# Block sums of the normalised x1 made before its transposition, all FFN-in tiles as seven block products

## The chip, the cores and the metric

The program runs on one core of one Trainium2 chip. The metric is the device time of one execution in microseconds. Engines: PE (TensorE), DVE (VectorE), ACT (ScalarE), POOL (GpSimd), SP (SyncE, which issues the DMAs here).

## What is computed

One encoder layer with 1024 tokens, model width 1024 and hidden width 2816, all fp32. The part of the reference that the change touches begins where the mixers (`mix`: four matrix-memory heads and eight window-attention heads) are done:

```python
x = _layer_norm(ALPHA * x + mix, ln1_g, ln1_b)          # x1
gate_ff, up_ff = jnp.split(x @ w_ffn_in, 2, axis=-1)
ffn = (jax.nn.silu(gate_ff) * up_ff) @ w_ffn_out
ple = jax.nn.sigmoid(x @ w_ple_gate) * (p_i @ w_ple_proj)
return _layer_norm(ALPHA * x + ffn + ple, ln2_g, ln2_b)
```

with `mix = concat(heads) @ w_out`, ALPHA = 2^(1/4) and `_layer_norm(x, g, b) = (x - mean) / sqrt(var + 1e-5) * g + b` over the 1024 columns.

## The kernel before, in words

Every matrix product is exact to fp32 by pieces: an operand is split into a high part (cast by ACT to fp32r, `..h` or `..hi`) and a low part (the remainder, subtracted by DVE or POOL, `..l` or `..lo`), and `mm3` (L110) issues three PE products, high x high, high x low and low x high. All products of this part have 512 columns. `split` makes the parts of one tile (L89); `load_w` loads a weight and splits it.

Stages, in order of time: projections and the two kinds of heads; the output projection (`out_proj`, PSUM banks named `yo`), which adds to eight token tiles y of 128x1024; the first norm; the FFN's inward products; the gate with its embedding product; the FFN's outward products; the second norm.

The output projection runs in two halves: the attention half under the last heads, the other at their end, 12 PE products for each token tile and half of the columns. After the second half of a tile, `ln1_norm` (L711) takes its statistics, ACT normalises, DVE multiplies by g1, POOL adds b1 (L722), and y goes to DRAM as `yd`, from where it is read again at the gate. `ln1_tr` (L726) transposes the tile on PE, 128x128 pieces into a bank `x1t`, eight for a token tile, and splits four columns' blocks into `x1h` and `x1l` (L741, L742).

The inward products have 22 tiles of 128 hidden columns (gate and up). The first two (NPL = 2) are plain: `ffn_plain` (L812), 16 products x 3 for each half of the tokens, 96 a tile, PSUM banks `fi`. The other twenty use a 2 x 2 block scheme (rows: halves of the tokens; inner: halves of x1's columns) with seven block products, 84 PE products a tile (`ffn_wino`, L881). Its operands are the blocks b11, b21, b22 of x1 itself, four block sums t1 to t4 that are made once, and sums of weight blocks that are made for each tile (`wino_w`, pieces a1 to a4). The sums t1 to t4 come from `diff` (L830): three DVE or POOL instructions of 128x1024 on the high and low parts already made, a cast and a remainder, beside the plain tiles' products. The results go to hidden blocks `ya` to `yd`, summed and written to DRAM for the outward stage; `weight_sums` (L791) does the like for the outward weights.

The gate is a seven-product scheme too, in the order 1, 2, 7, 6, 5, 3, 4 (MORDER). Its weight pieces `g<m><q>` come from raw tiles `wpg` by `piece` (L975), in products 3, 5, 6 and 7 after a sum of two raw tiles (`block_sum`, L970: q = 0 on DVE, q = 1 on POOL). `embed` (L1016) multiplies the embedding pieces `pu` (`p0`, `p1`) and `wu` (`wpp0`, `wpp1`) into one of three PSUM banks `plp` and has DVE multiply and add to the y read again.

Within an engine instructions run in program order; a scheduler sets that order when the program is built, by dependences and its own estimate of the time, so that the code's order is only a start. SBUF tiles come from tagged pools (X: 16 of 4 KB a partition; Y: 8; F4: 16; `raw`: 2; `whi`, `wlo`: 4), and a tile waits for the last reader of the slot that it takes.

## Time and profile before

| | |
|---|---|
| median of 3 runs | 1291.14 us (1290.29 to 1291.2) |
| the profiled execution | 1289.46 us, span in the trace 1287.7 us |
| PE busy | 1232.6 us (96%), 5985 products |
| DVE, ACT, POOL busy | 853.8, 510.6, 404.9 us |
| mean granted clock | 0.982 of full speed |

The span is the time from the first to the last record of the trace; the profiled execution is a little longer than it. A row of a timeline has the start, the duration, the engine and line, the operation, and in brackets how long the engine was idle before it and what ended that. A product of 512 columns is listed with 0.39 us, but products overlap: the distance of two starts is what each takes of PE's time.

### The profile page before, as it was taken

What the parts mean: (1) busy time and instruction counts of PE and PEld (TensorE: products, weight loads), DVE (VectorE), ACT (ScalarE), POOL (GpSimd) and SP (SyncE); (2) the same over time, 40 slices, a digit from 0 to 9 for tenths busy, and PEclk for the clock granted to TensorE, in tenths of its full rate; (3) what the DMA queues carried; (4) which work ended last, traced back from release to release, by engine and by line L of the source; (5) the groups of instructions that cost most, each with busy time, mean ns of one, the idle gap of its engine ahead of it and who ended that gap; (6) DMA issues with size and microseconds to landing.
All of it is one profiled execution on the core that took longest, in us unless ns stands there. A gap on an engine that the chain in (4) does not pass through costs nothing.

```text
span 1287.7 us, 16350 instructions
## 1 busy us (share of the span) xinstructions
PE 1232.6 (96%) x5985; PEld 1015.9 (79%) x5985; DVE 853.8 (66%) x1512; ACT 510.6 (40%) x906; POOL 404.9 (31%) x292
## 2 busy tenths in 40 slices
...
GB/s 240 115 36 66 46 54 50 151 34 87 90 177 221 49 102 111 34 106 130 173 203 188 167 130 212 172 188 166 161 136 199 165 179 229 180 191 197 151 1 131
DMA packets 67744, 174.39 MB, mean 135 GB/s; under 512 B 6288, under 2 KB 11088, under 8 KB 67664
## 3 DMA queue, kind: packets, MB, share of 16 engines
...
## 4 chain that ended last, share of the span: by engine, by line
PE 76%; DVE 12%; DMA 4%; POOL 3%; issue 2%; ACT 2%; SPq 1%; POOLq 0%; ACTq 0%; DVEq 0%
PE ma L113 5%; PE ma L111 5%; PE ma L112 5%; PE mc L111 3%; PE mc L112 3%; PE mc L113 3%; PE op L491 2%; PE oa L113 2%; PE oa L111 2%; PE oa L112 2%; PE ob L113 2%; PE ob L112 2%; PE ob L111 2%; PE pj_qk L111 2%; PE pj_qk L112 2%
## 5 line engine op out<-in xcount | busy, mean ns | idle before, releaser
L926 DVE TENSOR_TENSOR us<-us,ma 128x512 f32<-128x512 f32 x20 | 13.7, 686 | 103.3 <-PE ma L113 92.6
L1142 POOL TENSOR_TENSOR rs<-rs,mhalf 128x1 f32<-128x1 f32 x8 | 9.4, 1184 | 224.8 <-DVE rs L1141 224.6
L466 POOL TENSOR_SCALAR e<-e,st 128x384 f32<-128x384 f32 (+1 forms) x64 | 36.1, 577 | 119.2 <-DVE st L464 96.0
L865 POOL TENSOR_TENSOR s<-ru,rg 128x512 f32<-128x512 f32 x19 | 26.2, 1377 | 147.5 <-DMA ru<-in_wffi_dram 136.9
L462 ACT ACTIVATE e<-e,st 128x384 f32<-128x384 f32 (+1 forms) x64 | 37.2, 582 | 39.6 <-DVE st L458 39.5
L111 PE MATMUL yo<-hi_wo,mh 128*128 128x512 f32 x128 | 50.7, 396 | 1.9 <-DVE y L662 1.0
L111 PE MATMUL pj_qk<-xh,hi_qk 128*128 128x512 f32 x128 | 50.9, 398 | 0.0
L112 PE MATMUL pj_qk<-xl,hi_qk 128*128 128x512 f32 x128 | 50.9, 398 | 0.0
L113 PE MATMUL pj_qk<-xh,lo_qk 128*128 128x512 f32 x128 | 50.6, 395 | 0.0
L112 PE MATMUL yo<-lo_wo,mh 128*128 128x512 f32 x128 | 50.4, 395 | 0.0
L113 PE MATMUL yo<-hi_wo,ml 128*128 128x512 f32 x128 | 50.0, 395 | 0.0
L456 DVE CUSTOM_DVE_ANT_0 e<-sp,bias 128x384 f32<-128x384 f32 (+1 forms) x64 | 32.2, 521 | 24.5 <-PE sp L455 23.3
L870 POOL TENSOR_TENSOR s<-rg,s 128x512 f32<-128x512 f32 x20 | 28.6, 1432 | 60.8 <-DVE a4l L96 60.8
L874 POOL TENSOR_TENSOR s<-ru 128x512 f32<-128x512 f32 x20 | 32.7, 1633 | 45.4 <-DVE a2l L96 45.4
L283 DVE SCALAR_TENSOR_TENSOR qk<-pre,colt,qk 128x1024 f32<-128x1024 f32 x32 | 45.9, 1435 | 0.4
L90 ACT CAST a2h<-s 128x512 fp32r<-128x512 f32 x40 | 22.9, 618 | 46.9 <-PE mc L112 46.9
L90 ACT CAST a4h<-s 128x512 fp32r<-128x512 f32 x20 | 12.4, 621 | 69.6 <-PE ma L112 40.5
L111 PE MATMUL mc<-t1h,a3h 128*128 128x512 f32 x80 | 32.3, 403 | 4.3 <-ACT a3h L90 4.3
L491 PE MATMUL op<-eT,av 128*64 128x128 f32 x352 | 34.4, 285 | 0.0
L586 POOL TENSOR_TENSOR mw<-mw,maskb 128x512 f32<-128x512 f32 x16 | 24.1, 1504 | 32.7 <-DMA mw<-mwd 32.7
L113 PE MATMUL mc<-t1h,a3l 128*128 128x512 f32 x80 | 32.2, 403 | 1.6 <-DVE a3l L96 1.6
L113 PE MATMUL ma<-t2h,a2l 128*128 128x512 f32 x80 | 31.4, 392 | 0.8 <-DVE a2l L96 0.8
...
## 6 DMA issues: line engine op xcount, KB each, us to landing
...
```

The source lines that it names most:

```text
L90: act.copy(dst_hi, src)
L111: pe.matmul(o, ah, bh, start=start, stop=False, skip_group_check=goes_on)
L112: pe.matmul(o, ah, bl, start=False, stop=False, skip_group_check=goes_on)
L113: last["mm"] = pe.matmul(o, al, bh, start=False, stop=stop, skip_group_check=goes_on)
L283: dve.scalar_tensor_tensor(y, pre[:, w:w + S], colt[:, ct, w:w + 1], y, ALU.mult, ALU.add)
L456: dve.tensor_tensor_reduce(e[:, i, :L], sp[:, :L], biasd[j][:, i, off:off + L], 1.0, -BIG, ALU.add, ALU.max, accum_out=st[:, i:i + 1])
L462: act.activation(e[:, i, :L], e[:, i, :L], AF.Exp, bias=st[:, i:i + 1], accum_out=st[:, 2 + i:3 + i])
L466: pool.tensor_scalar(e[:, i, :L], e[:, i, :L], st[:, 6 + i:7 + i], 0.0, ALU.mult, ALU.add)
L491: pe.matmul(op[i * 64:i * 64 + 64, (n % 4) * P:(n % 4 + 1) * P], av[:, k0 + kb, i * 64:i * 64 + 64], eT[:, i, kb * P:(kb + 1) * P], start= ...
L865: (dve if i == NPL else pool).tensor_tensor(s3, ru[:, lo, :], rg[:, lo, :], ALU.subtract)
L870: pool.tensor_tensor(s4, rg[:, up, :], s2, ALU.subtract)
L874: pool.tensor_tensor(s1, ru[:, lo, :], ru[:, up, :], ALU.add)
```

## The change

In the change, all 22 inward tiles are done by seven block products, the first two as well, and the plain tiles' code goes. The tiles are normalised in the order 0, 1, 4, 5, 2, 3, 6, 7. POOL no longer adds b1 to y. The bias is a column constant when x1 is transposed: `bcol` (b1 as 128 x 8, columns on partitions) is added to b11, b21, b22 and t2 in the split (ACT with a bias, DVE with an instruction that adds and subtracts), and a difference of two of its halves to t3. t1 and t4 need none, since it cancels there. The block sums are made on y itself, in place, with y1 of token tile t and y2 of tile t + 4 (`t_sums`): for tiles 0 and 1 by POOL, for tiles 2 and 3 two of four by DVE. They wait for the write of y to `yd` and for the transposes of the blocks that the same y still has to give. The sums are then transposed (`tr_block`) like the blocks. The bias is put back onto the y read again: ALPHA x b1, 16 additions of POOL in the gate's stage.

The weights of tiles 0 and 1 load during the norm. Products 1 and 2 of tile 0 are issued ahead of the late sums. Raw tiles of the outward weights move from X to F4, behind a copy that holds each back (`weight_load`). In the gate, the raw tiles of products 1 and 2 load and the pieces of product 1 are made within the last inward tile; `wpp0` and `p0` go to Y slots, `p1` and `wpp1` to X.

```diff
-NPL = 2
+TORD = (4, 5, 0, 1, 6, 7, 2, 3)
+LORD = (0, 1, 4, 5, 2, 3, 6, 7)
...
-    section("F", {"xt": 2, "fo": 3})
+    section("F", {"w": 5})
...
+    bcol = const.tile([P, 8], F32, name="bcol")
+    nc.sync.dma_start(bcol, ln1b.rearrange("o (k p) -> p (o k)", p=P))
+    bdif = const.tile([P, 4], F32, name="bdif")
+    dve.tensor_tensor(bdif, bcol[:, 0:4], bcol[:, 4:8], ALU.subtract)
...
-            pool.tensor_tensor(ys, ys, b1a[:, nh * 512:nh * 512 + 512], ALU.add)
         nc.sync.dma_start(yd[t], y)
...
+    def tr_block(ts, k0, blk, tt, bias=None, late=False):
+        s = slice(tt * P, (tt + 2) * P)
+        for q in range(2):
+            tb = pjb("x1s") if late else bank("x1t", "w")
+            for j in range(2):
+                for i, t in enumerate(ts):
+                    c = k0 + (2 * q + j) * P
+                    pe.transpose(tb[:, (2 * j + i) * P:(2 * j + i + 1) * P], ya[t][:, c:c + P], ident)
+            h, l = blk[q]
+            if bias is None:
+                tv = tb.rearrange("p (a b) -> p a b", b=2 * P)
+                act.copy(h[:, :, s], tv)
+                dve.tensor_tensor(l[:, :, s], tv, h[:, :, s].bitcast(F32), ALU.subtract)
+                continue
+            for j in range(2):
+                tv, bc = tb[:, j * 256:j * 256 + 256], bias[:, 2 * q + j:2 * q + j + 1]
+                act.activation(h[:, j, s], tv, AF.Identity, bias=bc)
+                dve.scalar_tensor_tensor(l[:, j, s], tv, bc, h[:, j, s].bitcast(F32), ALU.add, ALU.subtract)
...
+    def t_sums(tt, late=False):
...
+        for t in (tt, tt + 1):
+            y1, y2 = ya[t], ya[t + 4]
+            eng = dve if late else pool
+            eng.tensor_tensor(y2[:, lohi[1]], y2[:, lohi[0]], y2[:, lohi[1]], ALU.subtract)
+            eng.tensor_tensor(y2[:, lohi[0]], y2[:, lohi[0]], y1[:, lohi[0]], ALU.subtract)
+            pool.tensor_tensor(y1[:, lohi[0]], y1[:, lohi[0]], y2[:, lohi[1]], ALU.subtract)
+            pool.tensor_tensor(y1[:, lohi[1]], y1[:, lohi[1]], y1[:, lohi[0]], ALU.subtract)
+        tr_block((tt + 4, tt + 5), 0, bx["t1"], tt, None, late)
+        tr_block((tt + 4, tt + 5), 512, bx["t3"], tt, bdif, late)
+
+    def t_sums_late():
+        bx["t2"], bx["t4"] = new_block((X, X), "t2"), new_block((F4, X), "t4")
+        for tt in (0, 2):
+            tr_block((tt, tt + 1), 0, bx["t2"], tt, b_hi, True)
+        for tt in (0, 2):
+            tr_block((tt, tt + 1), 512, bx["t4"], tt, None, True)
...
+    for n, t in enumerate(LORD):
+        for nh in range(2):
+            list(out_proj(t, nh, (0, 1), u, False))
         ln1_norm(t)
...
+        if n in (2, 4, 6):
+            ln1_tr(LORD[n - 2])
+        if n == 3:
+            ws = [wino_w1(0, raw8), wino_w1(1, raw8f)]
+        if n == 5:
+            t_sums(0)
+    ln1_tr(6)
...
+    def weight_load(r, after):
+        if r < NPR:
+            wsr[r] = F4([P, 2, 512], F32, f"sa{r}"), F4([P, 2, 512], F32, f"sb{r}")
+            for nh in range(2):
+                dve.tensor_copy(wsr[r][nh][:, 0, 0:1], after[:, 0:1])
+                nc.sync.dma_start(wsr[r][nh], wffo[r, nh])
...
-    def ffn_plain(i, w, hf):
...
-    def diff(new, plus, minus, name, engs, stage):
...
+    bs = {1: bx["b11"], 2: bx["b21"], 3: bx["b22"], 5: bx["t1"], 7: bx["t3"]}
+    w2 = {0: wino_w2(0, *ws[0])}
+    early = [wino_a(0, ws[0][2])]
+    t_sums(2, True)
+    early.append(wino_a(1, ws[1][2]))
...
+        if i == FT - 1:
+            load_gate(0, 0, F4)
+            load_gate(0, 1, lambda shape, dt, name: staging(shape, name))
+            m1g.append(piece(wpair, rawg[0, 0][0], 2, "g10", dve))
+        wino_b(i, w, *early[i])
+        if i == FT - 1:
+            m1g.append(piece(wpair, rawg[0, 0][1], 2, "g11", dve))
...
+        if m == 2:
+            load_gate(1, 1, F4)
+            wu[0] = load_h(ypair, wpp[0], "wpp0", dve)
+            pu[0] = load_h(ypair, pT[0], "p0", dve)
+            reload(range(4), Y)
...
-        if m == 2:
-            wu[0] = load_h(fpair, wpp[0], "wpp0", dve)
-            pu[0] = load_h(fpair, pT[0], "p0", dve)
         if m == 7:
             gs["v"] = temps(F4, "pv")
-            pu[1] = load_h(fpair, pT[1], "p1", pool)
...
+            for tt in range(4):
+                add_bias(0, 0, tt)
```

`wino_a` issues products 1 and 2 of a tile, `wino_b` the other five; for tile 0 it holds, between products 5 and 6, `t_sums_late`.

What the scheduler makes of it is seen at three places. On PE, at the end of the projection (`yo`), before: the last token tile is transposed, and the plain products of the first token half follow at once.

```order
L111 MATMUL yo<-hi_wo_4322,mh_4082 128x512
L112 MATMUL yo<-lo_wo_4323,mh_4082 128x512
L113 MATMUL yo<-hi_wo_4322,ml_4083 128x512
L737 MATMUL x1t<-ident,y_4060 128x128 x8
L111 MATMUL fi<-x1h_4478,hi_fi_4834 128x512
L111 MATMUL fi<-x1h_4478,hi_fi_4841 128x512
L112 MATMUL fi<-x1l_4479,hi_fi_4834 128x512
L113 MATMUL fi<-x1h_4478,lo_fi_4835 128x512
```

After: the last product's place is taken by transposes of several tiles (y_4108 is the last but one to be normalised), and the first block products, `mb` and `ma`, read b21 and b11, with the low parts from DVE.

```order
L112 MATMUL mb<-b21h_4458,a1h_4544 128x512
L739 MATMUL x1t<-ident,y_4144 128x128
L739 MATMUL x1t<-ident,y_4160 128x128
L739 MATMUL x1t<-ident,y_4144 128x128
L739 MATMUL x1t<-ident,y_4160 128x128
L113 MATMUL mb<-b21l_4459,a1h_4544 128x512
L114 MATMUL mb<-b21h_4458,a1l_4545 128x512
L739 MATMUL x1t<-ident,y_4108 128x128
L112 MATMUL mb<-b21h_4458,a1h_4544 128x512
L739 MATMUL x1t<-ident,y_4108 128x128
L112 MATMUL ma<-b11h_4454,a1h_4544 128x512
```

The first consumers behind the projection were products of one token half with plain weights, and are now those of two blocks that hold the tiles 2 and 3.

On DVE, at the same place, before: the last normalised tiles' multiplications (L721) and splits (L742).

```order
L717 SCALAR_TENSOR_TENSOR rs_4744<-mv_4743,rs_4744 128x1
L721 TENSOR_TENSOR y_4144<-y_4144,g1a 128x512 x2
L742 TENSOR_TENSOR x1l_4703<-x1t,x1h_4702 128x2x128
L742 TENSOR_TENSOR x1l_4705<-x1t,x1h_4704 128x2x128
L742 TENSOR_TENSOR x1l_4707<-x1t,x1h_4706 128x2x128
L717 SCALAR_TENSOR_TENSOR rs_4790<-mv_4789,rs_4790 128x1
L742 TENSOR_TENSOR x1l_4709<-x1t,x1h_4708 128x2x128
L721 TENSOR_TENSOR y_4160<-y_4160,g1a 128x512 x2
L742 TENSOR_TENSOR x1l_4703<-x1t,x1h_4702 128x2x128
```

After: the low parts of b11, b21 and t3 (L749), with weight pieces (L97) and the multiplications (L725) of the tile y_4108 between them.

```order
L725 TENSOR_TENSOR y_4108<-y_4108,g1a 128x512 x2
L97 TENSOR_TENSOR a2l_4867<-s_4872,a2h_4866 128x512
L749 SCALAR_TENSOR_TENSOR b11l_4455<-x1t,bcol,b11h_4454 128x256
L718 BN_AGGR mv_4819<-st_4802 128x2
L749 SCALAR_TENSOR_TENSOR b21l_4459<-x1t,bcol,b21h_4458 128x256
L749 SCALAR_TENSOR_TENSOR t3l_4667<-x1t,bdif,t3h_4666 128x256
L749 SCALAR_TENSOR_TENSOR t3l_4669<-x1t,bdif,t3h_4668 128x256
L749 SCALAR_TENSOR_TENSOR b11l_4457<-x1t,bcol,b11h_4456 128x256
L719 TENSOR_SCALAR rs_4820<-mv_4819 128x1
L749 SCALAR_TENSOR_TENSOR b21l_4459<-x1t,bcol,b21h_4458 128x256
L749 SCALAR_TENSOR_TENSOR b21l_4461<-x1t,bcol,b21h_4460 128x256
```

Weight pieces, gain multiplications and low parts of the sums now stand in one queue ahead of the last parts of b21.

On DVE in the gate, before: three sums of raw gate tiles (L973) and a piece of product 6 stand ahead of the low parts of `p0`.

```order
L978 TENSOR_TENSOR g70lo<-wpg_8012,g70hi 128x1024
L973 TENSOR_TENSOR wpg_8012<-wpg_8012,wpg_8016 128x1024
L973 TENSOR_TENSOR wpg_8004<-wpg_8004,wpg_8012 128x1024
L973 TENSOR_TENSOR wpg_8008<-wpg_8008,wpg_8012 128x1024
L978 TENSOR_TENSOR g60lo<-wpg_8012,g60hi 128x1024
L96 TENSOR_TENSOR p0lo<-r_p_8158,p0hi 128x512
L96 TENSOR_TENSOR p0lo<-r_p_8162,p0hi 128x512
L926 TENSOR_TENSOR e_8166<-pc_8080,pg_8094 128x512
```

After: the low parts of `p0` stand ahead of the three sums (L983), and the first multiplication by `plp` (L1071) behind them.

```order
L988 TENSOR_TENSOR g70lo<-wpg_8087,g70hi 128x1024
L97 TENSOR_TENSOR p0lo<-r_p_8165,p0hi 128x512
L97 TENSOR_TENSOR p0lo<-r_p_8169,p0hi 128x512
L965 TENSOR_TENSOR e_8241<-pc_8143,pg_8189 128x512
L983 TENSOR_TENSOR wpg_8087<-wpg_8087,wpg_8149 128x1024
L983 TENSOR_TENSOR wpg_7993<-wpg_7993,wpg_8087 128x1024
L983 TENSOR_TENSOR wpg_7997<-wpg_7997,wpg_8087 128x1024
L965 TENSOR_TENSOR e_8253<-pc_8143,pg_8190 128x512
L988 TENSOR_TENSOR g60lo<-wpg_8087,g60hi 128x1024
L1071 TENSOR_TENSOR e_8241<-e_8241,plp 128x512
```

The sums and `g60lo` keep their order among themselves; the embedding pieces and one addition have moved ahead of them.

## Rows read from the trace of the kernel before

**Rows 1.** PE's timeline, first norm to first seven-product tiles: start us, us, engine line operation
```profile
454.83 0.50 PE L111 MATMUL yo<-hi_wo,mh 128*128 128x512 f32 x1 [0.26 <-DVE y L662]
...
465.89 0.39 PE L113 MATMUL yo<-hi_wo,ml 128*128 128x512 f32 x1
...
477.00 0.39 PE L111 MATMUL yo<-hi_wo,mh 128*128 128x512 f32 x1
...
494.74 1.03 PE L737 MATMUL x1t<-ident,y 128*128 128x128 f32 x8
495.53 0.48 PE L112 MATMUL yo<-lo_wo,mh 128*128 128x512 f32 x1
...
579.01 0.63 PE L111 MATMUL mc<-t1h,a3h 128*128 128x512 f32 x1
...
582.42 0.63 PE L113 MATMUL mc<-t1h,a3l 128*128 128x512 f32 x1
...
600.40 0.39 PE L111 MATMUL mc<-t1h,a3h 128*128 128x512 f32 x1
```

**Rows 2.** Windows: stretch, its us, busy (x instructions) of PE PEld DVE ACT POOL, clock, DMA
```profile
570.00:600.00 30.00, 23.38 (x88) 17.94 (x87) 27.09 (x25) 10.66 (x17) 17.31 (x8) 0.83 0.42 151
600.00:970.00 370.00, 370.00 (x1634) 306.55 (x1633) 223.70 (x286) 127.92 (x207) 109.38 (x74) 1.00 0.49 172
```

**Rows 3.** Waits of PE over the whole run: total us, times, longest us
```profile
PE plp L113 <- DVE p0lo L96: 4.5, 1, 4.5
...
PE mc L111 <- ACT a3h L90: 4.3, 1, 4.3
...
PE x1t L737 <- DVE x1l L742: 3.0, 2, 1.5
PE pg L111 <- ACT g21hi L977: 2.8, 1, 2.8
```

**Rows 4.** PE's timeline in the gate
```profile
970.09 0.39 PE L113 MATMUL pg<-g20hi,x1l 128*128 128x512 f32 x1
...
992.90 0.64 PE L113 MATMUL plp<-wpp0hi,p0lo 128*128 128x512 f32 x1 [4.55 <-DVE p0lo L96]
...
997.35 0.39 PE L111 MATMUL pg<-g70hi,t3h 128*128 128x512 f32 x1
```

**Rows 5.** Groups of POOL, 456 to 600 us: count, busy us, mean ns
```profile
L722 POOL TENSOR_TENSOR y<-y,b1a 128x512 f32<-128x512 f32 x16 | 22.4, 1414 | 10.5 <-DVE y L721 10.5
```

**Rows 6.** Groups of DVE, 456 to 600 us
```profile
L721 DVE TENSOR_TENSOR y<-y,g1a 128x512 f32<-128x512 f32 x16 | 13.8, 883 | 1.4 <-ACT y L720 1.4
L742 DVE TENSOR_TENSOR x1l<-x1t,x1h 128x256 fp32r<-128x256 f32 x32 | 12.7, 412 | 4.5 <-ACT x1h L741 4.3
...
L662 DVE TENSOR_TENSOR y<-y,yo 128x512 f32<-128x512 f32 x15 | 10.2, 683 | 5.2 <-PE yo L113 5.1
L838 DVE TENSOR_TENSOR t1s<-t1s,x1l 128x1024 f32<-128x1024 f32 x2 | 6.7, 3412 | 0.0
...
L96 DVE TENSOR_TENSOR a1l<-rg,a1h 128x1024 fp32r<-128x1024 f32 x2 | 3.0, 1475 | 1.9 <-ACT a1h L90 1.9
L717 DVE SCALAR_TENSOR_TENSOR rs<-mv,rs 128x1 f32<-128x1 f32 x8 | 2.9, 368 | 4.2 <-POOL rs L716 4.2
...
L837 DVE TENSOR_TENSOR t2s<-t2s,x1l 128x1024 f32<-128x1024 f32 x2 | 2.4, 1210 | 0.0
```

**Rows 7.** The page's costliest groups: the projection's products
```profile
L111 PE MATMUL yo<-hi_wo,mh 128*128 128x512 f32 x128 | 50.7, 396 | 1.9 <-DVE y L662 1.0
```

**Rows 8.** DVE's timeline in the first 45 us
```profile
25.63 2.46 DVE L260 TENSOR_SCALAR bias<-nr 128x384 f32<-128x384 f32 x1
```

**Rows 9.** DVE's timeline in the gate
```profile
976.84 9.93 DVE L973 TENSOR_TENSOR wpg<-wpg,wpg 128x1024 f32<-128x1024 f32 x3
986.69 3.41 DVE L978 TENSOR_TENSOR g60lo<-wpg,g60hi 128x1024 fp32r<-128x1024 f32 x1
```

**Rows 10.** POOL's timeline in the gate
```profile
979.10 9.91 POOL L973 TENSOR_TENSOR wpg<-wpg,wpg 128x1024 f32<-128x1024 f32 x3
```

More of the change, by code (lines that the diff above doesn't have):

```diff
@@ L677, in out_att @@
         for nh in range(2):
-            for t in range(NT):
+            for t in TORD:
                 if nh == 0:
@@ new lines, in hybrid_layer @@
+    bx = {}
+    lohi = slice(0, 512), slice(512, 1024)
+    b_lo, b_hi = bcol[:, 0:4], bcol[:, 4:8]
+    def ln1_tr(t):
+        tt = t % 4
+        if t == 0:
+            bx["b11"], bx["b21"] = new_block((F4, F4), "b11"), new_block((F4, F4), "b21")
+        if t == 4:
+            bx["b22"] = new_block((F4, F4), "b22")
+        if t < 4:
+            tr_block((t, t + 1), 0, bx["b11"], tt, b_lo)
+            tr_block((t, t + 1), 512, bx["b21"], tt, b_hi)
+        else:
+            tr_block((t, t + 1), 512, bx["b22"], tt, b_hi)
@@ new lines, in t_sums_late, with wino_w1 @@
+    def t_sums_late():
[4 more added lines that the diff above has]
+            tr_block((tt, tt + 1), 512, bx["t4"], tt, None, True)
+    def wino_w1(i, new):
+        rg, ru = new(f"rg{i}"), new(f"ru{i}")
+        nc.sync.dma_start(rg, wffi[i, 0])
+        nc.sync.dma_start(ru, wffi[i, 1])
+        p1 = w_pair(i, 1)
+        split(flat(p1[0]), flat(p1[1]), flat(rg), dve)
+        return rg, ru, p1
@@ L876, in wino_w, with prod, wino_a @@
         halves(p3, lo, ru[:, up, :])
-        return (p1, 0), (p1, 4), (p2, 4), (p3, 0), (p3, 4), (p2, 0), (p4, 0)
+        return {3: (p2, 4), 4: (p3, 0), 5: (p3, 4), 6: (p2, 0), 7: (p4, 0)}
     us = {}
-    def ffn_wino(i, w):
+    def prod(w, m, o, first):
+        (pr, k0), bb = w[m], bs[m]
+        for kt in range(4):
+            q, j = divmod(kt, 2)
+            mm3(o, pr[0][:, k0 + kt, :], pr[1][:, k0 + kt, :], bb[q][0][:, j, :], bb[q][1][:, j, :],
+                first and kt == 0, kt == 3, not first)
+    def wino_a(i, p1):
         r, k = divmod(i, 2)
@@ L985, in fpair, with load_raw, load_gate, reload @@
         return [F4([P, 2, 512], F32R, f"{name}{c}") for c in ("hi", "lo")]
+    def load_raw(new, src, name):
+        t = new([P, 2, 512], F32, name)
+        nc.sync.dma_start(t, src)
+        return t
+    rawg = {}
+    def load_gate(nh, k, new):
+        rawg[nh, k] = [load_raw(new, wpg[nh, 2 * k + q], f"wpg{nh}{k}{q}") for q in range(2)]
+    m1g = []
+    bs = {1: bx["b11"], 2: bx["b21"], 3: bx["b22"], 5: bx["t1"], 7: bx["t3"]}
[3 more added lines that the diff above has]
+    early.append(wino_a(1, ws[1][2]))
+    summed = 0
+    for i in range(FT):
+        if i > 1:
+            ws.append(wino_w1(i, raw8))
+            early.append(wino_a(i, ws[i][2]))
+        w = w2[0] if i == 0 else wino_w2(i, *ws[i])
+        if i == FT - 1:
[5 more added lines that the diff above has]
+            m1g.append(piece(wpair, rawg[0, 0][1], 2, "g11", dve))
+        if i % 2:
+            hidden_sums(i // 2)
+        if i == 1:
+            weight_load(0, early[i][0])
+        while summed < min(NPR, (i - 1) * 2 // 3):
+            weight_sums(summed)
+            summed += 1
+            weight_load(summed, early[i][0])
+    ya = [None] * NT
+    def reload(ts, new):
+        for t in ts:
+            ya[t] = new([P, D], F32, f"x1{t}")
+            nc.sync.dma_start(ya[t], yd[t])
     def run(o, units, tts=range(4)):
```

194 lines of the change are left out of this document (62 added, 132 removed).

## The prediction

> **What bounds the kernel now.** I read the timeline of TensorE's products first, since PE is busy for 96% of the span, then the list of what PE waited for, then the windows with the granted clock, and last the groups and timelines of the engines that release PE. The reader is to see three things. Where PE has its operands, a product of 512 columns starts every 0.2267 us: from the row at 465.89 to that at 477.00 there are 49 steps in 11.11 us [rows 1]. Between 600 and 970 us PE never stops and the granted clock is 1.00 [rows 2]; the change leaves that stretch as it is, tile for tile, so nothing is to be had there. Time is lost in two places alone, and both are in the diff: from the first norm to the second of the seven-product tiles, and in the first half of the gate.
>
> Call F the stretch from the first `yo` product after the `tr` transposes, 454.83, to the first product of t1 with tile 3's weights, 600.40: 145.57 us [rows 1]. It holds 180 `yo` products, 192 `fi` products of the two plain tiles and 120 of tiles 2 and 3, so 492 x 0.2267 = 111.5 us, and 64 transposes at 0.099 us (eight between 494.74 and 495.53 [rows 1]), 6.3 us. The rest, 27.7 us, is loss: waits, of which [rows 3] has the largest, and products at half clock. Between 579.01 and 582.42 eight steps take 3.41 us, 0.427 us each [rows 1]; the windows there give a granted clock of 0.83 for 570 to 600 [rows 2]. A stall that long is followed by some 17 products at 1.2 instead of 2.4 GHz, each 0.20 us late: 3.4 us.
>
> The gate's stretch runs from 970.09 to 997.35, 27.26 us for 55 steps, which take 12.5 at full pitch [rows 4]: 14.8 us lost. Its waits are `g21hi` 2.8 and `p0lo` 4.5 [rows 3], the rest is smaller waits and the clock.
>
> **Products and transposes.** The first two tiles had 96 products each and get 84: 24 fewer, 24 x 0.2267 = -5.4 us. The block sums are now transposed too, seven blocks of 16 transposes each instead of eight token tiles of 8: 112 for 64, 48 x 0.099 = +4.75 us. Both lie on PE, so on the path: -0.7 us. That the change would remove more than that from PE is not in it.
>
> **The first norm and the first block products.** The addition of b1 leaves POOL (16 x 1.414 us [rows 5]) and the 128x1024 sums on DVE and POOL go. POOL gets 16 sums of 128x512, less four that DVE makes. POOL's sums of tiles 0, 1, 4, 5 are due after the write of y to `yd` and after the transposes of b11, b21 and b22, and nobody on PE wants them before the seventh product, so I take them at nothing; without that cover they cost 8 x 1.41 = 11.3 us. What counts is DVE. Before, the plain tile 0 needed only the split of one token half, and the sums (t1s at 3.41 and t2s at 1.21 us an instruction [rows 6]) ran beside 192 products that did not need them. Now the first product after `yo` reads b11 and b21 of tiles 2 and 3, which are normalised last, and nothing else stands before it on PE. By the order of the changed kernel DVE has in its queue, from the second addition of tile 3 to the last low part of b21: five additions of 128x512 at 0.683 and five statistics of that size, priced like them (6.8 us), 16 splits of 128x256 out of PSUM at 0.412 (6.6), two a1l at 1.475 (3.0), five other 128x512 low parts at 0.68 (3.4), four gain multiplications at 0.883 (3.5) and nine small ones at up to 0.37 (3.3): 26.6 us [rows 6]. Tile 3's second product ends near 489: 454.83 + 132 x 0.2267 + 24 transposes + the 1.9 us of early waits on `y` that the page lists for `yo` [rows 7]. So b21 is whole at 489 + 26.6 = 515.6. PE has done the last `yo` at 489 + 48 x 0.2267 + 2 = 502 and the transposes behind it at 504. It stalls for 11.6 us, and 3.4 more go in the clock.
>
> Next, tile 1's products run, and the sums of tiles 2, 3, 6, 7 have to be made, transposed and split before product 5: a chain of DVE, POOL, PE, ACT and DVE. I price its stall like the one before at the same product (`a3h`, 4.3 [rows 3]) with its 3.4 of clock; last, t2 and t4 go through three PSUM banks, each freed by a split, priced like the wait of the transposes for a bank before, 3.0 [rows 3]. New loss: 1.9 + 11.6 + 3.4 + 4.3 + 3.4 + 3.0 = 27.6, against 27.7: the stretch gives 0.1, and 0.7 with PE's work. Bounds: if DVE never falls behind, only the early waits, 3.0 for a bank and one stall with its clock stay, 12 us; if the DVE instructions with two SBUF operands run at the slow rate of t1s (3.41 against 1.21, 2.8 times) beside POOL's sums, the queue grows by the length of POOL's sums, 11.3 us, to a loss of 39.
>
> On that last point the traces show t1s at 3.41 us while POOL made t3s, and t2s, the same size, at 1.21 [rows 6]. The Trainium skill (SBUF — State Buffer, "SBUF: two separate sides") says that a DVE instruction with two SBUF inputs and a GpSimd instruction that reads SBUF exclude each other for a whole instruction, and that DVE with one SBUF input is free of it. The trace agrees in size. By it the new splits out of PSUM escape, a1l, the other low parts and the gain multiplications don't, and the low part of b21 would come some 4 to 5 us later, at about 520: an estimate of mine, which would bring the sum to 1286.
>
> The load of `bcol`, in pieces of four bytes, is new and no row shows such a transfer. DVE's `bdif` waits for it ahead of `bias`, which ran at 25.63 [rows 8] after two multiplications and has some 3 us until the gates. I take 0; 4 is the upper end, if it lands at twice the delay of its neighbours. The early loads of the weights of tiles 0 and 1 and the gated loads into F4 replace loads that the trace never waits for; 0, and 3 as the upper end (a bank's wait of [rows 3]).
>
> **The gate.** Before, DVE's three block sums (9.93 us from 976.84) and `g60lo` (3.41) stand ahead of both `p0lo` [rows 9], and POOL's three sums (9.91) run at the same time [rows 10]. PE, at `plp` since 988, waited for `p0lo` until 992.90 [rows 3, 4]. Now the `wpp0` and `p0` pieces go to Y slots and their low parts stand ahead of the three sums, and the raw pieces of product 2 are loaded behind the last tile's weights: `p0lo` and `g21hi` are no longer late. What is late next: `plp` has three PSUM banks, the fourth group waits for the first multiplication by `plp` on DVE, and that one stands behind the three sums and `g60lo`, 13.3 us of work that starts when product 2 ends. PE reaches the fourth group after three groups of six products and what else stands there, some 9 us. Stall about 4, and 2.5 of clock: 6.5 lost instead of 14.8, a gain of 8.3. Bounds: nothing lost (DVE's sums at 1.21 each since POOL's come earlier) and 12 lost (the sums as slow as now, PE there early): gain 14.8 to 2.8. The 16 additions of the bias on POOL, 16 x 1.41 = 22.6 us, lie in the gate's second half and under the output stage; the bound is one of them, 1.4, on the path.
>
> **Sum.** -0.8 - 8.3 = -9.1, against the profiled execution of 1289.46 (span 1287.70 and 1.76 around it): 1280.4. The median shown is 1.68 above that execution, so 1282.
>
> **Rivals.**
> A, slower: DVE is the bound of the first block products. Between the end of `yo` and the last low part, DVE's queue is 15 us longer than summed: the multiplications, a1l, a4l and a2l (8.5 us) at 2.8 times their time beside POOL. Loss 27.6 + 15 = 42.6, F gives -14.9 + 0.7, the gate 8.3: +5.9, 1297. It decides from a queue 11.7 us longer on (b21 whole after 527). For it: t1s at 3.41. Against it: POOL has only 11.3 us of sums, and half of DVE's queue reads PSUM. 0.16.
> B, next to no change: the three sums still end last in the gate, with nothing gained but the early wait of 2.8, and F stays as it is: 1291.14 - 2.8 - 0.8 = 1287.5; with a late `bcol` or load 1291. For it: DVE's order keeps the sums ahead of the release of `plp`. Against it: PE gets there with work left. 0.12.
> C, nearly all stalls go: DVE keeps up with `yo`, as it did with 80 instructions in the norm, F's loss falls to 12 and the gate's to 2: -15.7 - 0.7 - 12.8 = -29, 1262. For it: an addition out of PSUM takes DVE 0.683 us, a quarter of the 2.7 that PE needs for its 12 products, so DVE can catch up between them; against: 26.6 us of queue in 13 us of `yo`. 0.22.
> The forecast, 1270 to 1288: 0.50.
>
> **How the numbers follow.** The range takes in the forecast, B, most of C from 1264 on and the near part of A up to 1296; the forecast's own range is 1270 to 1288. A measurement of this kernel tells 0.2%, 2.6 us, from no change. Faster: 0.50 + 0.22 + 0.02 of B = 0.74; same: the rest of B, 0.10; slower: A, 0.16.
>
> **What would show it.** Right: PE idle after the last `yo` for 8 to 15 us, ended by a low part of b21 at 513 to 518, then two shorter stalls before t1 and t2; no wait for `p0lo`, and one for a `plp` bank of some 4 us; F at 143 to 147 us. A shows as b21 after 527, B as a `plp` wait over 8 us, C as products without a gap behind `yo`. A wait in the first 40 us for `bcol`, or one on weights of tile 0, would make the prediction wrong from a side that I priced at nothing.

## The result, and the profile after

The changed kernel takes 1269.99 us (median of four runs, 1267.67 to 1271.32) against 1290.72 for the kernel before, run beside it: a ratio of 0.9842 (95% interval 0.9821 to 0.9862), 20.7 us faster. The same kernel run again later gave 1269.64 against 1290.18, 0.984 (0.9825 to 0.9855). The forecast was 1282, with a range of 1264 to 1296: the direction held and the time lies in the range, but the gain is more than twice the 9.1 us that I had summed.

Where it came from is read best from three starts on PE: the first `yo` product behind the `tr` transposes, the first product with `g10hi`, and the first with `g50hi`. Between them lie F with the even stretch behind it, the first part of the gate, and the rest.

| from, to | before | after, first profile | after, second profile |
|---|---|---|---|
| start of the span to first `yo` | 454.83 | 453.90 | 454.98 |
| `yo` to `g10` (F and the even stretch) | 491.01 | 483.34 | 485.02 |
| `g10` to `g50` (gate) | 71.93 | 58.71 | 58.41 |
| `g50` to the end | 269.93 | 269.95 | 269.99 |
| span | 1287.70 | 1265.9 | 1268.4 |

The first profile is of the fastest run, the second (1270.16 us) of one near the median, so the second is used for sizes: the gate gave 13.5 us, F 6.0, and nothing else moved by more than 0.2. That is 19.3 between these two profiles, of 20.7 between the medians. First the busy times from the page of the first profile, with the number of instructions.

```profile
PE 1223.8 (97%) x6009; PEld 1011.4 (80%) x6009; DVE 848.8 (67%) x1549; ACT 520.0 (41%) x928; POOL 395.2 (31%) x297
```

PE has 6009 records for 5985, which is the -24 products and +48 transposes of the sum. The windows of that profile that answer to [rows 2] (busy time of PE, PEld, DVE, ACT, POOL, then the granted clock, DMA share and GB/s):

```profile
570.00:600.00 30.00, 30.00 (x134) 24.84 (x133) 15.80 (x23) 9.67 (x16) 8.38 (x6) 1.00 0.52 176
600.00:970.00 370.00, 370.00 (x1634) 306.36 (x1633) 246.66 (x314) 135.01 (x216) 115.05 (x75) 1.00 0.51 176
```

The stretch from 600 to 970 is full in both kernels; what is gone is the loss from 570 to 600 (23.38 us busy, clock 0.83 in [rows 2]). Its new losses lie earlier, behind the last `yo`. PE's waits over the run, which answer to [rows 3] (those before 450 us are left out):

```profile
PE x1t L739 <- DVE t1l L744: 3.1, 1, 3.1
PE x1s L739 <- DVE y L780: 3.0, 1, 3.0
PE mb L112 <- ACT b21h L748: 2.4, 1, 2.4
PE x1t L739 <- DVE mv L718: 1.6, 1, 1.6
PE pg L112 <- DVE e L965: 1.2, 1, 1.2
PE yo L112 <- DVE y L663: 1.1, 2, 0.8
```

The waits for `p0lo` and `g21hi` are gone, and the gate has one wait of 1.2 us. And PE's timeline behind the last `yo`, which answers to [rows 1]:

```profile
500.60 0.40 PE L114 MATMUL yo<-hi_wo,ml 128*128 128x512 f32 x1
504.09 1.97 PE L739 MATMUL x1t<-ident,y 128*128 128x128 f32 x8 [3.09 <-DVE t1l L744]
508.41 0.80 PE L112 MATMUL mb<-b21h,a1h 128*128 128x512 f32 x1 [2.36 <-ACT b21h L748]
510.83 1.08 PE L739 MATMUL x1t<-ident,y 128*128 128x128 f32 x4 [1.62 <-DVE mv L718]
511.57 0.77 PE L113 MATMUL mb<-b21l,a1h 128*128 128x512 f32 x1
...
524.76 1.54 PE L739 MATMUL x1s<-ident,y 128*128 128x128 f32 x6 [3.00 <-DVE y L780]
```

PE does starve behind `yo`, but in pieces, with transposes between them, and the first product that reads a low part of b21 starts at 511.57.

### The profile page after: what moved, and what is told of

It reads as the page before. It is cut to its first block, busy times and chain, and to the rows that moved or that the text cites. A ratio compares the mean times of both kernels' runs of the same rounds, so it can differ in the third digit from the quotient of the medians.

```text
span 1265.9 us, 16488 instructions
## 1 busy us (share of the span) xinstructions
PE 1223.8 (97%) x6009; PEld 1011.4 (80%) x6009; DVE 848.8 (67%) x1549; ACT 520.0 (41%) x928; POOL 395.2 (31%) x297
## 4 chain that ended last, share of the span: by engine, by line
PE 85%; DVE 7%; DMA 2%; ACT 2%; POOL 2%; issue 2%; POOLq 0%; SPq 0%; DVEq 0%; ACTq 0%
PE ma L113 6%; PE ma L112 6%; PE ma L114 6%; PE mc L113 3%; PE mc L114 3%; PE mc L112 3%; PE op L492 2%; PE oa L113 2%; PE oa L112 2%; PE oa L114 2%; PE ob L113 2%; PE ob L112 2%; PE ob L114 2%; PE yo L112 2%; PE yo L114 2%; PE yo L113 2%
## 5 line engine op out<-in xcount | busy, mean ns | idle before, releaser
L897 POOL TENSOR_TENSOR s<-ru,rg 128x512 f32<-128x512 f32 x22 | 29.5, 1343 | 187.1 <-DMA ru<-in_wffi_dram 185.3
L906 POOL TENSOR_TENSOR s<-ru 128x512 f32<-128x512 f32 x22 | 37.4, 1701 | 39.2 <-DVE a2l L97 39.2
L91 ACT CAST a2h<-s 128x512 fp32r<-128x512 f32 x44 | 26.2, 620 | 52.4 <-PE mc L113 36.6
L112 PE MATMUL mb<-b21h,a1h 128*128 128x512 f32 x88 | 35.0, 398 | 2.4 <-ACT b21h L748 2.4
L874 DVE TENSOR_TENSOR sa<-sb,sa 128x512 f32<-128x512 f32 x11 | 8.3, 752 | 43.3 <-DMA sb<-in_wffo_dram 43.3
L960 DVE TENSOR_TENSOR yb<-yb,us 128x512 f32<-128x512 f32 x22 | 37.0, 1683 | 0.3 <-ACT yb L959 0.3
L112 PE MATMUL ma<-t2h,a2h 128*128 128x512 f32 x88 | 34.6, 394 | 1.3 <-ACT a2h L91 0.7
L898 POOL TENSOR_TENSOR s<-s,ru 128x512 f32<-128x512 f32 x22 | 32.6, 1484 | 9.8 <-DVE a3l L97 8.2
```

The lines of the kernel that those rows point to most:

```text
L91: act.copy(dst_hi, src)
L112: pe.matmul(o, ah, bh, start=start, stop=False, skip_group_check=goes_on)
L897: pool.tensor_tensor(s3, ru[:, lo, :], rg[:, lo, :], ALU.subtract)
L898: pool.tensor_tensor(s2, s3, ru[:, up, :], ALU.add)
L906: pool.tensor_tensor(s1, ru[:, lo, :], ru[:, up, :], ALU.add)
L960: dve.tensor_tensor(hb_, hb_, u, ALU.mult)
```

## Experiments: the gate

**b_y.** The kernel before, with one part of the change alone: `wpp0` and `p0` go to Y slots, and half of the reloaded y goes to X to make room. With that, the two loads and the reads of y stand at another place in the code.

```diff
+        if m == 2:
+            wu[0] = load_h(ypair, wpp[0], "wpp0", dve)
+            pu[0] = load_h(ypair, pT[0], "p0", dve)
+            reload(range(4), Y)
+        if m == 6:
+            reload(range(4, 8), X)
...
-        if m == 2:
-            wu[0] = load_h(fpair, wpp[0], "wpp0", dve)
-            pu[0] = load_h(fpair, pT[0], "p0", dve)
```

> The kernel before with one part of the change alone: wpp0 and p0 go to Y slots (x1's second half is read again into X slots), nothing else. Theory G (the slot of the embedding operands decides the gate: in F4 slots they wait for product 1 of the gate to release a block of x1, and only then come the low parts, behind DVE's three sums): the wait for p0lo goes, and with it most of the 14.8 us lost in the gate; the gate's stretch is 11 to 14 us shorter, 1277 to 1280 in all. Rival L (the earlier raw loads of product 2 and the early pieces of product 1 are half of it): only the p0lo wait of 4.5 and its 2 to 3 of half-clock products go, 1283 to 1285, and the wait for g21hi of 2.8 stays. Rival S (the sums only move the wait on to the plp banks, as the prediction had it): a plp wait of about 4 and its clock, 1283 or more.

Measured: 1275.49 us, ratio 0.9891 (0.9876 to 0.9905), so 14.5 us of the gain; its gate took 57.58 us (71.93 before) and its F 490.91 (491.01). What held the pieces before stands on ACT, whose timeline I had not read. Before:

```profile
970.29 1.14 ACT L90 CAST wpp0hi<-r_wpp 128x512 fp32r<-128x512 f32 x2 [3.38 <-PE pg L112]
972.22 1.04 ACT L977 CAST g21hi<-wpg 128x1024 fp32r<-128x1024 f32 x1 [0.79 <-DMA wpg<-in_wpg_dram]
...
985.67 1.14 ACT L90 CAST p0hi<-r_p 128x512 fp32r<-128x512 f32 x2 [4.41 <-PE pg L112]
```

And ACT in b_y:

```profile
955.34 1.13 ACT L90 CAST wpp0hi<-r_wpp 128x512 fp32r<-128x512 f32 x2
960.84 1.05 ACT L982 CAST g21hi<-wpg 128x1024 fp32r<-128x1024 f32 x1 [4.38 <-DMA wpg<-in_wpg_dram]
...
962.97 0.62 ACT L90 CAST p0hi<-r_p 128x512 fp32r<-128x512 f32 x1
```

Before, the casts `wpp0hi` and `p0hi` each waited for a PE product of the gate, 3.38 and 4.41 us: their F4 slots were held by what product 2 still read (not product 1, as I had expected). `g21hi`, for which PE waits 2.8 us in [rows 3], stood behind the waiting `wpp0hi`; but its row names a DMA, and ACT sat idle for 0.79 us more until the raw tile had landed. So that wait ended with the DMA, and the slot alone does not explain it. The queue of SyncE, before and then in b_y, shows what was issued ahead of the tile (`x<-yd` is y read again):

```profile
956.88 1.86 SPq L955 DMA_DIRECT2D x<-yd  x4
...
961.61 2.97 SPq L1013 DMA_DIRECT2D wpg<-in_wpg_dram  x3
...
971.66 0.94 SPq L1007 DMA_DIRECT2D r_p<-in_pT_dram  x2
```

```profile
957.17 0.42 SPq L1018 DMA_DIRECT2D wpg<-in_wpg_dram  x1
958.72 0.33 SPq L1012 DMA_DIRECT2D r_p<-in_pT_dram  x1
...
963.16 7.28 SPq L957 DMA_DIRECT2D x<-yd  x4
```

Before, the reads of y went ahead of three raw tiles of the gate and of `p0`'s raw tiles; in b_y they come behind. `p0hi` did wait for its slot last, and `p0lo` stands behind the three sums [rows 9], which is PE's wait of 4.5. With Y slots neither cast waits for PE. DVE in b_y:

```profile
965.37 1.28 DVE L96 TENSOR_TENSOR p0lo<-r_p,p0hi 128x512 fp32r<-128x512 f32 x2
966.75 5.82 DVE L978 TENSOR_TENSOR wpg<-wpg,wpg 128x1024 f32<-128x1024 f32 x3
972.49 0.68 DVE L926 TENSOR_TENSOR e<-pc,pg 128x512 f32<-128x512 f32 x1
```

`p0lo` now stands ahead of the sums, and these take 5.82 instead of 9.93 us. DVE's order, which the forecast treated as the cause, changed with this edit. So b_y shows that slots, code order and the reads of y together are worth 14.5 us; how much each of them is worth was not run.

**b_yraw.** b_y, and also the raw tiles of product 2 into the staging slots, as the change has them.

```diff
-    for (nh, k), new in (((0, 0), X), ((0, 1), X), ((1, 0), staging), ((1, 1), F4)):
+    for (nh, k), new in (((0, 0), X), ((0, 1), staging), ((1, 0), X), ((1, 1), F4)):
```

> As b_y, and product 2's raw tiles load into the staging slots (product 6's into X), so early. Theory G: within 1.5 us of b_y. Rival L: 3 to 6 us below b_y, at 1277 to 1280.

Measured: 1275.39 us, 0.989 (0.9876 to 0.9905), gate 58.53. No more than b_y: the other slots for the raw tiles are worth nothing on top of it. Putting the embedding operands back into F4 in the changed kernel wasn't tried.

In the changed kernel the same rows of DVE, which answer to [rows 9]:

```profile
957.10 1.28 DVE L97 TENSOR_TENSOR p0lo<-r_p,p0hi 128x512 fp32r<-128x512 f32 x2
959.20 0.69 DVE L965 TENSOR_TENSOR e<-pc,pg 128x512 f32<-128x512 f32 x1 [0.82 <-PE pg L114]
964.27 5.82 DVE L983 TENSOR_TENSOR wpg<-wpg,wpg 128x1024 f32<-128x1024 f32 x3 [4.39 <-DMA wpg<-in_wpg_dram]
...
970.61 2.83 DVE L988 TENSOR_TENSOR g60lo<-wpg,g60hi 128x1024 fp32r<-128x1024 f32 x1
973.37 1.27 DVE L1071 TENSOR_TENSOR e<-e,plp 128x512 f32<-128x512 f32 x2
```

And the two rows of PE that answer to [rows 4]:

```profile
974.18 0.41 PE L112 MATMUL plp<-wpp0hi,p0hi 128*128 128x512 f32 x1
...
978.36 0.50 PE L112 MATMUL pg<-g70hi,t3h 128*128 128x512 f32 x1 [1.25 <-DVE e L965]
```

The multiplication that frees a `plp` bank starts at 973.37, and PE's fourth group follows at 974.18 without a wait.

## Experiments: the first block products

**after2.** The changed kernel again, no edit, beside the kernels below.

> The changed kernel once more, for a second profile and more times of it: the first profile was of its fastest run. Expected 1268 to 1271, the gate's stretch (first product 1 to first product 5) within 1 us of 58.7, and the stretch from the projection to the gate 483 to 487.

Measured: 1269.64 us (1268.92 to 1270.67), F 485.02. All sizes of F below are against this one.

**f_heavy.** Six statistics of 128x512 more on DVE, while the late tiles are normalised.

```diff
         nc.sync.dma_start(yd[t], y)
+        if t == 3:
+            for nh in (0, 1, 0, 1, 0, 1):
+                dve.bn_stats(dmy, y[:, nh * 512:nh * 512 + 512])
```

> The changed kernel with six more statistics instructions of 128x512 (about 0.69 us each, 4.1 in all, result unused) on DVE after the multiplication of tile 3, so in the queue ahead of the last low parts of b21. Theory D (DVE's queue sets when the first block products can go on): 3 to 5 us slower than the changed kernel, 1273 to 1275, and the first low part of b21 3 to 4 us later. Rival B (PSUM banks and ACT's splits set it, DVE has room): within 1.5 us of the changed kernel.

Measured: 1273.99 us, 0.988 (0.9863 to 0.9896); F 488.36, 3.3 us longer. The last low part of b21 on DVE, in the changed kernel (first profile) and then in f_heavy:

```profile
510.72 0.43 DVE L749 SCALAR_TENSOR_TENSOR b21l<-x1t,bcol,b21h 128x256 fp32r<-128x256 f32 x1
...
513.71 0.48 DVE L749 SCALAR_TENSOR_TENSOR b21l<-x1t,bcol,b21h 128x256 fp32r<-128x256 f32 x1 [0.48 <-ACT b21h L748]
```

```profile
513.56 0.47 DVE L753 SCALAR_TENSOR_TENSOR b21l<-x1t,bcol,b21h 128x256 fp32r<-128x256 f32 x1
...
517.79 0.48 DVE L753 SCALAR_TENSOR_TENSOR b21l<-x1t,bcol,b21h 128x256 fp32r<-128x256 f32 x1 [0.48 <-ACT b21h L752]
```

4.1 us of work (six at 0.68) made the last part of b21 later by 3.4 us than in the first profile and by 2.9 than in the second (515.30), each counted from its own first `yo`, and the time 4.3 us longer. Work added to DVE's queue there is on the path.

**f_light, f_pool, f_late.** Three ways to take DVE's work out of that place: the weights of tile 1 load behind the norm; the two a1l go to POOL; the transposes of the sums of tiles 0, 1, 4, 5 come behind those of b11 and b21.

```diff
# f_light
-            ws = [wino_w1(0, raw8), wino_w1(1, raw8f)]
+            ws = [wino_w1(0, raw8)]
...
     t_sums(2, True)
+    ws.append(wino_w1(1, raw8f))
# f_pool
-        split(flat(p1[0]), flat(p1[1]), flat(rg), dve)
+        split(flat(p1[0]), flat(p1[1]), flat(rg), pool if i < 2 else dve)
# f_late
+        if late:
+            t_tr(tt, late)
+
+    def t_tr(tt, late):
         tr_block((tt + 4, tt + 5), 0, bx["t1"], tt, None, late)
         tr_block((tt + 4, tt + 5), 512, bx["t3"], tt, bdif, late)
...
+    t_tr(0, True)
     t_sums(2, True)
```

> The changed kernel with the weights of tile 1 loaded and split after the late sums instead of during the norm: one a1l of 128x1024 (1.65 us) less in DVE's queue ahead of b21. Theory D: 1.5 to 2.5 us faster than the changed kernel, 1268, with the first low part of b21 earlier by that much. Rival B: no difference beyond 0.5 us. If the weights of tile 1 then come late, a new wait on a1 in tile 1, and 1271 or more.

> The changed kernel with the low parts a1l of tiles 0 and 1 (3.8 us of DVE in its trace) made by POOL. Theory D: b21 up to 3.8 us earlier, 1266 to 1268, if POOL's sums of tiles 0 and 1, which end at 503, don't make a1l late. Rival N: within 1 us. A wait on a1l in the first product, and 1271 or more, if POOL is late.

> The changed kernel with the transposes and splits of t1 and t3 for tiles 0 and 1 (16 transposes; 2 t1l and 4 t3l, 3.0 us of DVE) moved behind those of b11 and b21 of tiles 2 and 3; POOL's sums stay where they are. Theory D (DVE's queue ahead of b21 sets the first block products): b21 comes 2 to 3 us earlier and the time falls by as much, 1267 to 1268. Rival N (the norm of the last tile, statistics, power on POOL, scale on ACT, sets it as much as the queue): less than 1 us. If product 5 then waits for t1, the gain comes back as a wait there: 1270.

Measured: 1270.03 (0.985, 0.9835 to 0.9866), 1271.67 (0.9856, 0.9842 to 0.9871) and 1270.91 us (0.9855, 0.9831 to 0.9878), F 484.86, 484.95 and 486.06. None gains. In f_light the scheduler moved the low parts of a3 up into the hole, so that DVE's queue was no shorter there. In f_pool part of the work came back on DVE: beside POOL's two a1l (2.38 and 2.36 us) an a4l took 2.73 and an a2l 2.01, against 1.15 and 0.68 in after2. What limits f_late was not isolated. More on DVE costs about its length, less gave nothing; which other chain is then the bound these three runs do not show.

**f_fill.** 24 products whose result nobody reads, on PE behind the last `yo`, to keep the clock up.

```diff
+    dm = pjb("dm")
+    for n in range(24):
+        pe.matmul(dm, mh[0, 0][:, 0, 0:P], u[0, 0][0][:, 0, :], start=n == 0, stop=n == 23)
     ln1_tr(6)
```

> The changed kernel with 24 products of 512 columns on PE whose sum nobody reads, 18 of them directly behind the last product of the projection and 6 behind eight transposes, where PE stands idle for 3.1 and 2.4 us now and then works at half clock until 514. Theory C (the clock after the idle time costs 2 to 3 us): the granted clock stays at 1.0 from 500 to 514 and the time falls by 1 to 3 us. Theory D (DVE's queue sets the end whatever PE's clock): within 1 us of the changed kernel, or slower by up to 1.5 where the extra products are longer than the idle time.

Measured: 1271.63 us (1266.15 to 1271.89), 0.9846 (0.9823 to 0.9869), F 486.78. The window from 500 to 514 us in f_fill, and then in the changed kernel (second profile):

```profile
500.00:514.00 14.00, 12.08 (x55) 9.49 (x54) 14.00 (x27) 9.64 (x21) 7.15 (x7) 0.89 0.22 76
```

```profile
500.00:514.00 14.00, 6.24 (x36) 4.73 (x35) 14.00 (x27) 7.95 (x17) 9.27 (x7) 0.78 0.29 105
```

PE was kept busy and the clock was granted at 0.89 instead of 0.78, and the time is no shorter. DVE is busy for all 14 us in both. But behind that window the clock is lower in f_fill, 0.80 against 0.85 from 514 to 540 us, and from 500 to 540 it is 0.83 in both. The fillers moved the slow stretch and did not remove it, so this run does not tell what the clock is worth there.

## Experiments: the bias

**f_bias2.** 16 additions of 128x512 back on POOL, in the place of those of b1, and nothing else. They add g1, so the values are other ones; the work is that of b1.

```diff
             dve.tensor_tensor(ys, ys, g1a[:, nh * 512:nh * 512 + 512], ALU.mult)
+            pool.tensor_tensor(ys, ys, g1a[:, nh * 512:nh * 512 + 512], ALU.add)
```

> The changed kernel with 16 additions of 128x512 by POOL put back into the norm (of g1 instead of b1, so the values are wrong; nothing else, the splits and slots as in the changed kernel). Theory K (POOL's addition in the chain of each tile costs PE time, by its 1.3 to 1.4 us and by holding DVE up): 3 to 6 us slower than the changed kernel, all of it between the projection and the gate. Rival V (f_bias was slower by its slots in the gate alone): within 1.5 us.

Measured: 1277.44 us, 0.99 (0.9886 to 0.9914), so 7.8 us of the gain are gone; F 491.62, as long as before the change, and the gate as in after2 (58.33). The windows of f_bias2, and then of after2:

```profile
500.00:510.00 10.00, 3.83 (x28) 2.91 (x27) 10.00 (x16) 4.59 (x10) 10.00 (x7) 0.98 0.14 54
510.00:520.00 10.00, 6.78 (x18) 4.00 (x17) 9.51 (x20) 6.50 (x14) 8.93 (x8) 0.50 0.18 52
```

```profile
500.00:510.00 10.00, 4.30 (x30) 3.26 (x28) 10.00 (x16) 6.41 (x14) 7.86 (x6) 0.90 0.28 95
510.00:520.00 10.00, 7.94 (x26) 6.10 (x26) 6.70 (x17) 3.99 (x8) 1.97 (x3) 0.59 0.26 105
```

With the additions POOL is busy for 18.9 of the 20 us, for 9.8 without. Two rows of POOL's timeline, from f_bias2 and then from after2, have its last sum of the tiles 0, 1, 4, 5:

```profile
511.24 1.28 POOL L783 TENSOR_TENSOR y<-y 128x512 f32<-128x512 f32 x1
```

```profile
500.01 4.49 POOL L782 TENSOR_TENSOR y<-y 128x512 f32<-128x512 f32 x2
```

It ends at 512.5 with the additions and at 504.5 without. Groups of DVE from 489 to 530 us in f_bias2 (count, busy us, mean ns), and then in after2:

```profile
L97 DVE TENSOR_TENSOR a2l<-s,a2h 128x512 fp32r<-128x512 f32 x2 | 3.5, 1756 | 0.0
...
L750 DVE SCALAR_TENSOR_TENSOR b21l<-x1t,bcol,b21h 128x256 fp32r<-128x256 f32 x4 | 1.9, 472 | 0.0
```

```profile
L749 DVE SCALAR_TENSOR_TENSOR b21l<-x1t,bcol,b21h 128x256 fp32r<-128x256 f32 x4 | 1.8, 464 | 0.5 <-ACT b21h L748 0.5
L97 DVE TENSOR_TENSOR a2l<-s,a2h 128x512 fp32r<-128x512 f32 x2 | 1.4, 678 | 0.0
```

The low part a2l, with two SBUF operands, takes 1.76 us beside the fuller POOL and 0.68 without; the splits of b21, which read one operand from PSUM, take 0.47 in both. The last b21l starts at 520.51 in f_bias2 and at 515.30 in after2:

```profile
520.51 0.47 DVE L750 SCALAR_TENSOR_TENSOR b21l<-x1t,bcol,b21h 128x256 fp32r<-128x256 f32 x1
```

```profile
515.30 0.48 DVE L749 SCALAR_TENSOR_TENSOR b21l<-x1t,bcol,b21h 128x256 fp32r<-128x256 f32 x1 [0.48 <-ACT b21h L748]
```

So b21 is whole 5.2 us later (4.8 counted from the first `yo`). The Trainium skill (SBUF — State Buffer, "SBUF: two separate sides") has a DVE instruction with two SBUF inputs and a GpSimd instruction that reads SBUF exclude each other. The rows of a2l agree, and those of b21l show a split with one SBUF input untouched. The hold is not the same for all: the two a1l took 1.28 us each in f_bias2 and 1.92 in after2, where POOL's sums of y ran beside them. Of the 6.6 us in F the waits of PE are the smaller part: they add up to 16.2 us here and to 13.6 in after2. Behind them PE works slower, at a granted clock of 0.75 from 500 to 540 us against 0.83.

**f_bias.** The bias put back as it was: POOL adds b1 in the norm, the splits are without a bias, and b1 takes an F4 slot again.

```diff
+    b1a = F4([P, D], F32, "b1a")
+    nc.sync.dma_start(b1a, ln1b.to_broadcast([P, D]))
...
+            pool.tensor_tensor(ys, ys, b1a[:, nh * 512:nh * 512 + 512], ALU.add)
...
-            if bias is None:
+            if True:
...
-            ab = F4([P, D], F32, "ab")
```

> The changed kernel with b1 added to y by POOL again, as before (16 of 1.41 us in the norm), the splits without a bias, and no addition in the gate. The chain from a tile's last product to its transposition gets two POOL instructions longer (2.8 us), and POOL's sums start later, but DVE's splits are half as many instructions (128x512 in place of two of 128x256: 0.69 for 0.86). Theory D with the last tile's chain behind the queue: 1 to 3 us slower, 1271 to 1273. Rival Q (the bias in the split is worth nothing, the chain has slack): within 1 us, or 1 us faster by the shorter queue.

Measured: 1275.74 us (1274.39 to 1277.62), 0.9893 (0.9875 to 0.9911); F 487.10, gate 61.96. It costs 6.1 us, but not in the same places: 2.1 in F and 3.5 in the gate. I take the gate's part for the slots of F4, which b1 shifts; that was not isolated. Without a bias the splits are also done as 128x512 at 0.68 us instead of two of 128x256 at 0.47, which shortens DVE's queue. So this run mixes three edits, and f_bias2 is the cleaner one.

**f_actchain.** The norm's chain made longer on ACT instead of POOL: 16 copies in place.

```diff
             dve.tensor_tensor(ys, ys, g1a[:, nh * 512:nh * 512 + 512], ALU.mult)
+            act.activation(ys, ys, AF.Identity)
```

> The changed kernel with 16 more instructions of ACT (a copy of y in place, 128x512, some 0.76 us) in the norm between DVE's multiplication and the transposition: each tile's chain is longer by about as much as half of POOL's addition of f_bias2 (1.48 us) plus the same hand-over, but POOL and its hold on DVE are left out. Theory C (f_bias2's 7.8 us come from the longer chain of each tile): 3 to 6 us slower than the changed kernel, 1273 to 1276. Theory L (they come from POOL's being busy: DVE instructions with two SBUF operands held up, POOL's power and sums later): within 1.5 us of 1269.6.

Measured: 1270.89 us (1269.87 to 1272.19), 0.9858 (0.9842 to 0.9875), F 484.66. The copies take 0.63 us each; F is no longer than in after2 (485.02), and the 1.3 us in the medians are within the two intervals. So a longer chain as such hardly costs, which speaks for POOL's being busy as the cause in f_bias2. A link as long as POOL's own (1.48) was not tried on ACT.

**f_sumslate.** The block sums of tiles 0, 1, 4, 5 made behind the norm, those of one column half on DVE.

```diff
-        if n == 5:
-            t_sums(0)
     ln1_tr(6)
+    t_sums(0, True)
```

> The changed kernel with the sums of tiles 0, 1, 4, 5 issued after the norm, four of the eight by DVE instead of POOL (2.7 us more in DVE's queue, 5.5 less on POOL beside it). Theory L: DVE's multiplications and weight parts run freer; 1 to 3 us faster than the changed kernel, 1267 to 1269. Theory C: DVE's longer queue costs 1 to 3 us, 1271 to 1273.

Measured: 1269.99 us, 0.9852 (0.9837 to 0.9866), F 484.64. Four of POOL's sums less in the norm give nothing more. The last b21l came 2.5 us earlier than in after2 (512.86 here, 515.30 there, each counted from its first `yo`), and F is no shorter: PE then waits again at the transposes of the late sums (`x1s <- DVE y`, 2.9 us). So b21 is on the path, but it is not the only bound of F.

**b_nobias.** b_y without POOL's 16 additions of b1, which leaves b1 out of x1.

```diff
-            pool.tensor_tensor(ys, ys, b1a[:, nh * 512:nh * 512 + 512], ALU.add)
```

> b_y without POOL's 16 additions of b1 in the norm (the addition of b1 is left out). Theory K: 2 to 5 us faster than b_y (1275.5), 1271 to 1273, so most of what the change gains in the norm. Rival M (the gain there comes from the block sums on y and the plain tiles' products): within 1.5 us of b_y.

Measured: 1273.23 us (1271.32 to 1275.49), 0.9871 (0.9854 to 0.9887), F 488.51. In the scheme of before the same 16 additions cost some 2.3 us (the two intervals overlap). With them the old scheme takes 1275.5 and the new one 1277.4; without them 1273.2 and 1269.6. By these four the new block scheme gains in F only when POOL is relieved; f_bias, with a shorter queue on DVE, softens that.

**b_npl1.** b_y with one plain tile instead of two, and the sums still made from the split parts.

```diff
-NPL = 2
+NPL = 1
```

> b_y with one plain inward tile instead of two: 12 products fewer (2.7 us), and 96 products less that hide the block sums of 128x1024 made after the transposition. Theory W (those sums need the cover; only making them on y lets the plain tiles go): PE waits some 10 to 20 us longer for t1 to t4, 1283 to 1293. Rival F (the sums had slack): 2 to 3 us faster than b_y, 1273.

Measured: 1290.73 us, 1.0 (0.9991 to 1.001), 15.2 us over b_y. PE's waits in it:

```profile
PE ma L111 <- ACT a1h L90: 14.7, 2, 14.3
PE ma L111 <- DVE us L926: 10.8, 1, 10.8
```

The first wait, up to 551.49, is for a weight piece, whose cast had waited 5.26 us for its raw tile; DVE had made sums and their low parts from 525.76 on. The second, up to 590.15, is for an addition that stood behind the sums t2 and t4 on DVE. So the plain tiles covered the old sums and the first weight pieces, and here a plain tile saved without moving the sums lost more than it gave.

No run beat the changed kernel beyond its interval.

## Why the prediction was right and wrong

**PE's work, -0.7.** Right by the count of records, and no more than that.

**The gate, -8.3: too small by 5.2; the measured gain is 13.5.** The waits that go were named rightly, and so was what stands behind them on DVE. The step that failed is "13.3 us of work that starts when product 2 ends" with its "Stall about 4, and 2.5 of clock: 6.5 lost". The first addition on DVE needs only the first token tile of product 2 (959.20); the sums followed at 964.27, when their raw tiles had landed and product 2 had some 3 us to go (its last product starts at 967.15), and with `g60lo` they took 9.2 us (964.27 to 973.44), not 13.3. PE came to the fourth group as its bank was free. What is left is one wait of 1.2. The bound "nothing lost", a gain of 14.8, was near the truth; I took a value in the middle, with the sums at 3.31 each [rows 9]. They took 5.82 in all: the first two, begun before POOL's own sums (965.66), 1.23 each, the third, beside them, 3.42. Which part of the edit of b_y moved the work forward stays open.

**F, -0.8: too small by 5.2; the measured gain is 6.0.** Two steps failed. The first is the stall: DVE's queue was forecast well (b21 whole at 515.6; measured 514.2 and 515.8 in the two profiles), and f_heavy shows that it counts, f_sumslate that it is not the only bound. (The tiles 2 and 3 are not "normalised last", as I wrote: 6 and 7 come behind them. The sum had them at the right place.) But "it stalls for 11.6 us" took PE to need the whole of b21 at once. Its first product needs a quarter: the first low part was ready at 511.15, PE used it at 511.57, and the products of b11 that came between covered the rest; up to there PE had waited 7.1 us in three pieces. PE's waits in F add up to some 13 us (1.1, 3.1, 2.4, 1.6, 3.0 in the rows above and four under 0.8) instead of 1.9 + 11.6 + 4.3 + 3.0 = 20.8. The price of the clock was not too large: of the loss of 27.7, 5.3 went beside PE's work, so 22.4 is left, and 9 of it is not waits, against 6.8 in the sum.

The second is the addition of b1 on POOL, of which I wrote only that it leaves, and which stands in the sum at nothing. f_bias2 prices it at 7.8 us with the new scheme: POOL's sums then stand in a full queue, the norm's power with them, and some of DVE's low parts from SBUF are held. How the price divides among these is not shown. The forecast carried POOL's hold on DVE as a loss to come from POOL's sums (b21 "at about 520"); it came to 520 only when the additions were put back. I had weighed the sums that POOL gets and not the additions that leave it. How the 6.0 divides between the scheme and the bias is not settled beyond that: f_bias2 gives back 6.6 in F, f_bias, with its cheaper splits, 2.1.

**What I took at nothing.** `bcol` cost nothing, as said: `bdif` ran at 25.07 without a wait, and `bias`, behind it, at 25.30 (25.63 in [rows 8]). The early loads of the weights cost nothing that a wait shows, and the 16 additions in the gate and the output stage left `g50` to the end as it was (269.99 to 269.93).

**The rivals.** A needed b21 after 527, and it came at 514 to 516, and at 520.5 in the worst case made. B needed a `plp` wait over 8 us; there was none. C was the nearest in the gate (2 lost there, 13.5 gained for its 12.8) and wrong in F, where waits of 13 us remain for its 12 of loss in all. The truth lies between the forecast and C: C's price was right for the gate, the forecast's was nearer in F.
